# Retention scores and cross terms on the two row halves of the array, 64 deep, instead of zero-padded pairs of heads

## The chip, the cores and the metric

The kernel runs on one core of a Trainium2 chip. The metric is the device time of one execution in microseconds (us). Below, PE is TensorE, DVE is VectorE, ACT is ScalarE, POOL is GpSimd, SP is the queue that issues most transfers. A "weight load" is the LDWEIGHTS in front of every matmul: it puts the stationary operand, up to 128 rows by 128 columns, into the array; the moving operand is then streamed through it, one column after the other.

## The reference, cut to what matters

A hybrid layer: a normalised input is projected, one half of the channels goes through a gated linear recurrence, the other half through chunkwise retention with 8 heads, and an output projection joins them. The change lies in the retention alone:

```python
# q, k: (chunks, 128, 8 heads, 64); v: (chunks, 128, 8 heads, 128)
s = jnp.einsum('bnchd,bnmhd->bnhcm', q, k) * dmask            # scores, inner dimension d = 64
inner = jnp.einsum('bnhcm,bnmhe->bnche', s, v)
kv = jnp.einsum('bnchd,bnche->bnhde', k_dec, v)
state = g_chunk * state + kv                                  # (8 heads, 64, 128), chunk after chunk
cross = jnp.einsum('bnchd,bnhde->bnche', q_dec, state_before) # inner dimension d = 64
o = inner + cross
```

Every product of scores and of cross terms sums over the 64 channels of one head, half of the 128 rows that the array has.

## The kernel before, in words

All large products are made in three passes of a rounded format (float32r): an operand is split into a high part (rounded by ACT) and a low part (the rest, by DVE), and `mm3` (L112 to L116) adds high by high, high by low and low by high into one PSUM bank. The kernel has three stages. Up to about 860 us it makes the recurrence (tiles `px`, `pg`, `pgt`). From there to about 2140 us comes the retention (L619 to L879), and then the output projection (`sweep`, L366).

The retention runs twice over 32 chunks of 128 positions (`for ph in range(2)`, four heads each time: 64 chunk steps in all). One step of the loop at L837 does, for chunk n and the one before it:

- `front_qk` (L696): 24 matmuls of 512 columns project q and k (`ps0`); `rope` (L674) rotates and scales them on DVE.
- `back_s` (L745) of the chunk before: the scores `pS`. `front_g` has transposed q and k, so that a pair of heads stands on the 128 partitions, head 0 on rows 0 to 63 and head 1 on rows 64 to 127. To keep the two heads apart with products of full depth, q was copied into padded tiles `qbh` and `qbl`, 128 rows by 2 x 128 columns, in which each head's rows are zero in the other head's columns. One `mm3` per pair makes 256 columns at once. DVE multiplies by the mask (`sm`, L752).
- `front_v` (L711) and `front_g` (L723): 24 matmuls each for v (`ps1`) and the gate (`ps2`), their copies out, the transposes of q and k by DVE (`pT`, L634), the split into `qh` and `ql`, and the padded copies by ACT (L739 to L742).
- `back_o` (L755): the output `po`. The cross terms are two `mm3` of 256 columns against the padded state `sbh`, `sbl`; the inner terms are four plain float32 products of the masked scores with v (L764), each of which shows as two passes in the trace. Then the chunk's k by v (`pkv`, six matmuls), the update of `state` on DVE (L776), its split by `state_parts` (L638), the statistics of the head norm (L782, L783) and the normalised output `on` (ACT, L791).
- `back_g`, `back_y` (L795, L799): the gate's multiplication, and four transposes `py` on PE.

PSUM has eight banks, two for each of the tags "a" to "d". `ps0` uses "a", `ps1` and `ps2` use "b", `pS` and `py` take turns on "c", and `po` and `pkv` on "d". A tile may be written when the last reader of the tile that had its bank before is done. The order of the instructions on an engine is made by a scheduler that plans with an estimated timeline; the program's text sets only dependences and priorities.

```python
pads: qbh, qbl, sbh, sbl = [P, 2, 2, P] float32r, set to 0 by POOL once (L623 to L628)
mm3(pS[:, 2 * p2:2 * p2 + 2, :], (qh[:, 2 + p2, :], ql[:, 2 + p2, :]), (qbh[:, p2], qbl[:, p2]), True, True)
```

Of the kernel before, what the change touches and what calls it, by code (L numbers as in the profile page):

```python
# [33 lines left out]
def hybrid_kernel(ctx: ExitStack, tc: tile.TileContext, xa, xt, x, meta, w_in, w_out,  # L34
# [584 lines left out]
    with ExitStack() as cd:  # L619
        tp = cd.enter_context(tc.tile_pool(name="cd_t", bufs=2, reuse_waits="tile"))  # L620
        kp = cd.enter_context(tc.tile_pool(name="cd_c", bufs=2, reuse_waits="tile"))

        pads = []  # L623
        for nm in ("qbh", "qbl", "sbh", "sbl"):
            t = kp.tile([P, 2, 2, P], F32R, name=nm, bufs=1)
            nc.gpsimd.memset(t.bitcast(F32), 0.0)
            pads.append(t)
        qbh, qbl, sbh, sbl = pads  # L628

        def transpose4(dst, src):  # L630
            sv = src.rearrange("p (a g e) -> p a g e", a=4, g=4)
# [4 lines left out]
            return ins  # L636

        def state_parts():  # L638
            for j in range(2):
                r = slice(64 * j, 64 * j + 64)  # L640
                nc.scalar.copy(out=sbh[r, :, j, :], in_=state[r])
                nc.vector.tensor_tensor(sbl[r, :, j, :], state[r], sbh[r, :, j, :].bitcast(F32), op=ALU.subtract)

        late = []
        for ph in range(2):
# [77 lines left out]
            def front_g(cur):  # L723
                n = cur["n"]
                pg = proj(2, cur["xs"])
                gs = tp.tile([P, 512], F32, tag="gs", name="gs")
                th = tp.tile([P, 512], F32, tag="th", name="th", bufs=1)
                hr = tp.tile([P, 1], F32, tag="hr", name="hr")
                nc.gpsimd.tensor_scalar(hr, rstd[:, n:n + 1], 0.5, None, op0=ALU.mult)
                nc.scalar.activation(th, pg, AF.Tanh, scale=hr)  # L730
                nc.scalar.activation(gs, pg, AF.Identity, scale=rstd[:, n:n + 1])
                nc.vector.scalar_tensor_tensor(gs, th, 1.0, gs, op0=ALU.add, op1=ALU.mult)
                cur["gs"] = gs
                pT = tp.tile([P, 4, P], F32, tag="pT", name="pT", bufs=1)
                cur["tr"] = transpose4(pT, cur["rd"].rearrange("p h d -> p (h d)"))
                qh = tp.tile([P, 4, P], F32R, tag="qh", name="qh")
                ql = tp.tile([P, 4, P], F32R, tag="ql", name="ql")
                split(pT, qh, ql)
                for j in range(2):  # L739
                    r = slice(64 * j, 64 * j + 64)  # L740
                    nc.scalar.copy(out=qbh[r, :, j, :], in_=pT[r, 0:2, :])
                    nc.scalar.copy(out=qbl[r, :, j, :], in_=ql[r, 0:2, :].bitcast(F32))  # L742
                cur["q"] = (qh, ql)

            def back_s(st):  # L745
                qh, ql = st["q"]
                pS = psp.tile([P, 4, P], F32, tag="c", name="pS")
                for p2 in range(2):
                    mm3(pS[:, 2 * p2:2 * p2 + 2, :], (qh[:, 2 + p2, :], ql[:, 2 + p2, :]),
                        (qbh[:, p2], qbl[:, p2]), True, True)  # L750
                sm = tp.tile([P, 4, P], F32, tag="sm", name="sm")
                nc.vector.tensor_tensor(sm, pS, msk.rearrange("p (h c) -> p h c", c=P), op=ALU.mult)  # L752
                st["sm"] = sm

            def back_o(st):  # L755
                n, sm, v, kn = st["n"], st["sm"], st["v"], st["kn"]
                qh, ql = st["q"]
                po = psp.tile([P, 4, VD], F32, tag="d", name="po")
                for p2 in range(2):
                    mm3(po[:, 2 * p2:2 * p2 + 2, :], (qh[:, p2, :], ql[:, p2, :]), (sbh[:, p2], sbl[:, p2]),  # L760
                        True, False)
                    for j in range(2):
                        h = 2 * p2 + j
                        nc.tensor.matmul(po[:, h, :], sm[:, h, :], v[:, h * VD:(h + 1) * VD],  # L764
                                         start=False, stop=(j == 1))
                if n < NT - 1:
                    vh, vl = st["vs"]
                    pkv = psp.tile([P, 2, 2, VD], F32, tag="d", name="pkv")
                    for p2 in range(2):
                        c = slice(p2 * 128, p2 * 128 + 128)  # L770
                        c2 = slice(p2 * 256, p2 * 256 + 256)
                        mm3(pkv[:, p2], (kn[:, 0, c], kn[:, 1, c]), (vh[:, c2], vl[:, c2]), True, True)
                    for p2 in range(2):
                        for j in range(2):
                            r = slice(64 * j, 64 * j + 64)
                            nc.vector.scalar_tensor_tensor(state[r, p2, :], state[r, p2, :], dc[r, 2, p2:p2 + 1],  # L776
                                                           pkv[r, p2, j, :], op0=ALU.mult, op1=ALU.add)
                    state_parts()
                mv = tp.tile([P, 4, 2], F32, tag="mv", name="mv")
                bs = tp.tile([P, 4, 6], F32, tag="bs", name="bs")  # L780
                for h in range(4):
                    nc.vector.bn_stats(bs[:, h, :], po[:, h, :])  # L782
                    nc.vector.bn_aggr(mv[:, h, :], bs[:, h, :])  # L783
                rs = tp.tile([P, 4], F32, tag="rs", name="rs")
                rsqrt_mean(rs, mv[:, :, 1], P, 4, 1.0)
# [2 lines left out]
                nc.gpsimd.tensor_scalar(nb, nb, -1.0, None, op0=ALU.mult)  # L788
                on = mp.tile([P, 4, VD], F32, tag="xlb", name="on")
                for h in range(4):  # L790
                    nc.scalar.activation(on[:, h, :], po[:, h, :], AF.Identity, bias=nb[:, h:h + 1],  # L791
                                         scale=rs[:, h:h + 1])
                st["on"] = on

# [167 lines left out]
```

## Time and profile before

| | |
|---|---|
| median of 3 runs | 2772.62 us (2769.89 to 2774.16) |
| the profiled execution | 2772.7 us |
| its span, first to last instruction | 2770.9 us |
| PE busy | 2716.7 us, 98% |
| DVE busy | 2130.1 us, 77% |
| ACT busy | 1374.0 us, 50% |
| POOL busy | 544.9 us, 20% |
| mean granted clock of TensorE | 0.994 of full speed |

Matmuls are pipelined: a record lasts longer than the matmul occupies the array, because the next one's record opens while it still drains. So the rows of the timeline are read by their starts: what one matmul costs is the distance from its start to the next one's. Where several records of one line follow one another, the timeline merges them into a row with a count (x8), its start and its whole length. "PEld" rows are weight loads; shapes are rows*columns of the stationary operand, then partitions x columns of the moving one.

### The profile page before, as it was taken

The numbers are of one execution on the slowest core, as the hardware profiler recorded it, in microseconds if no ns is written. First come the engines' busy times: TensorE is split into PE (matmuls) and PEld (weight loads), VectorE is DVE, ScalarE is ACT, GpSimd is POOL, SyncE is SP. The second block draws the span as 40 slices with busy tenths as digits, with TensorE's granted clock in tenths as the row PEclk, the third lists the DMA queues.
The fourth block names the chain that finished last, engine by engine and source line by source line (L and its number), as shares of the span: only waits on it lengthen the run. The fifth ranks groups of instructions, "written<-read, shape, count | busy, mean of one in ns | idle before, by whom it ended". The sixth has DMA issues, their size and how long they took to land.

```text
span 2770.9 us, 37027 instructions
## 1 busy us (share of the span) xinstructions
PE 2716.7 (98%) x13178; PEld 2288.6 (83%) x13178; DVE 2130.1 (77%) x4502; ACT 1374.0 (50%) x2451; POOL 544.9 (20%) x702
## 2 busy tenths in 40 slices
PE   7999999999999999999999999999999999999998
PEld 7788888888888888888888888888887888877886
DVE  7777889878789877777779888888778755566664
ACT  5766666655565444444446544454445422244342
POOL 3101021000003322222222222222221000012222
PEclk9999999999999999999999999999999999999999
DMA  6434334212224222222214222223112745475654
GB/s 197 120 106 121 118 97 122 84 57 67 75 85 145 72 69 72 69 72 69 70 57 164 79 80 83 101 109 114 47 48 77 191 112 111 108 206 162 178 158 116
DMA packets 164411, 290.10 MB, mean 105 GB/s; under 512 B 21201, under 2 KB 89330, under 8 KB 163714
## 3 DMA queue, kind: packets, MB, share of 16 engines
q1 hardware_dynamic: 150690, 238.45, 26.8%
q0 software_dynamic: 13536, 49.29, 8.2%
q8 instruction: 103, 1.69, 0.3%
q14 instruction: 82, 0.67, 0.1%
HBM read 205.87 MB, written 98.58 MB: 110 GB/s over the span
## 4 chain that ended last, share of the span: by engine, by line
PE 80%; DVE 9%; DMA 4%; issue 3%; ACT 2%; POOL 1%; SPq 0%; DVEq 0%; POOLq 0%; ACTq 0%
PE ps L114 12%; PE ps L116 12%; PE ps L115 12%; PE pg L114 3%; PE pg L116 3%; PE pg L115 3%; PE px L116 3%; PE px L114 3%; PE px L115 3%; PE po L764 2%; PE oc L295 2%; PE oc L297 2%; PE od L297 2%; PE oc L296 2%; PE od L296 2%
## 5 line engine op out<-in xcount | busy, mean ns | idle before, releaser
L114 PE MATMUL ps<-cwh,xhi 128*128 128x512 f32 x1536 | 605.7, 394 | 0.6 <-DVE mr L671 0.6
L116 PE MATMUL ps<-cwh,xlo 128*128 128x512 f32 x1536 | 600.4, 391 | 0.7 <-POOL xlo L180 0.7
L115 PE MATMUL ps<-cwl,xhi 128*128 128x512 f32 x1536 | 600.3, 391 | 0.0
L116 PEld LDWEIGHTS ps<-cwh,xlo 128*128 128x128 f32 x1536 | 288.9, 188 | 62.4 <-POOL xlo L180 1.1
L114 PEld LDWEIGHTS ps<-cwh,xhi 128*128 128x128 f32 x1536 | 289.2, 188 | 57.4 <-DVE mr L671 1.0
L115 PEld LDWEIGHTS ps<-cwl,xhi 128*128 128x128 f32 x1536 | 289.2, 188 | 55.8 <-issue 0.2
L634 DVE STREAM_TRANSPOSE pT<-rd 32x128 f32<-32x128 f32 x1024 | 310.0, 303 | 16.4
L180 POOL TENSOR_TENSOR xlo<-xraw,xhi 128x1024 fp32r<-128x1024 f32 x64 | 163.8, 2559 | 529.6 <-ACT xhi L179 523.6
L105 ACT ACTIVATE yop<-yraw 128x512 fp32r<-128x512 f32 x192 | 116.9, 628 | 217.6 <-DVE yraw L264 71.5
L114 PE MATMUL px<-xhi,lwh 128*128 128x512 f32 (+2 forms) x576 | 215.3, 375 | 8.3 <-ACT lwh L108 6.5
L114 PE MATMUL pg<-xhi,lwh 128*128 128x512 f32 (+2 forms) x576 | 212.8, 370 | 3.6 <-DVE sg L492 3.2
L116 PE MATMUL px<-xhi,lwl 128*128 128x512 f32 (+2 forms) x576 | 214.3, 372 | 1.0 <-DVE lwl L106 1.0
L116 PE MATMUL pg<-xhi,lwl 128*128 128x512 f32 (+2 forms) x576 | 212.4, 369 | 2.8 <-DVE lwl L109 1.7
L115 PE MATMUL px<-xlo,lwh 128*128 128x512 f32 (+2 forms) x576 | 213.9, 371 | 1.0 <-DVE xlo L106 0.9
L115 PE MATMUL pg<-xlo,lwh 128*128 128x512 f32 (+2 forms) x576 | 212.2, 368 | 0.0
L475 DVE SCALAR_TENSOR_TENSOR xc<-xlb,vec,xc 128x512 f32<-128x512 f32 (+2 forms) x216 | 155.4, 720 | 30.2 <-ACT xc L472 26.5
L106 DVE TENSOR_TENSOR yop<-yraw,yop 128x512 fp32r<-128x512 f32 x192 | 130.0, 689 | 52.6 <-ACT yop L105 50.7
L791 ACT ACTIVATE on<-po,nb,rs 128x128 f32<-128x128 f32 x256 | 96.3, 457 | 129.7 <-POOL nb L788 129.7
L782 DVE BATCH_NORM_STATS2 bs<-po 128x6 f32<-128x128 f32 x256 | 57.0, 285 | 108.0 <-PE po L764 107.9
L114 PEld LDWEIGHTS px<-xhi,lwh 128*128 128x128 f32 x576 | 110.5, 192 | 26.8 <-ACT lwh L108 6.5
L114 PEld LDWEIGHTS pg<-xhi,lwh 128*128 128x128 f32 x576 | 109.5, 190 | 22.3 <-DVE sg L492 4.3
L115 PEld LDWEIGHTS px<-xlo,lwh 128*128 128x128 f32 x576 | 110.6, 192 | 20.1 <-DVE xlo L106 1.9
(216 smaller groups left out, 6179.8 us busy)
## 6 DMA issues: line engine op xcount, KB each, us to landing
xraw<-in_xt_dram SPq DMA_DIRECT2D x64, 512.0 KB, 4.6
yraw<-ydram SPq DMA_DIRECT2D x64, 512.0 KB, 3.8
xraw<-in_xa_dram SPq DMA_DIRECT2D x56, 512.0 KB, 4.0
hdram<-in_x_dram SPq DMA_DIRECT2D x32, 512.0 KB, 3.9
xn<-in_x_dram SPq DMA_DIRECT2D x32, 512.0 KB, 5.3
ydram<-sg SPq DMA_DIRECT2D x256, 64.0 KB, 1.7
ydram<-yt SPq DMA_DIRECT2D x64, 256.0 KB, 2.4
hdram<-h POOLq DMA_DIRECT2D x32, 512.0 KB, 5.2
```

The source lines that it names most:

```text
L105: nc.scalar.activation(hi, src, AF.Identity)
L106: return nc.vector.tensor_tensor(lo, src, hi.bitcast(F32), op=ALU.subtract)
L114: nc.tensor.matmul(ps, ah, bh, start=start, stop=False)
L115: nc.tensor.matmul(ps, ah, bl, start=False, stop=False)
L116: nc.tensor.matmul(ps, al, bh, start=False, stop=stop)
L180: nc.gpsimd.tensor_tensor(lo, raw, hi.bitcast(F32), op=ALU.subtract)
L296: nc.tensor.matmul(ps, ah, bl, start=False, stop=False, skip_group_check=more)
L297: mm = nc.tensor.matmul(ps, al, bh, start=False, stop=k == 3, skip_group_check=more)
L475: conv = nc.vector.scalar_tensor_tensor(xc[:, :T], xl[:, j:j + T], vec[:, 6 + j, ch:ch + 1], xc[:, :T], op0=ALU.mult, op1=ALU.add)
L634: ins = nc.vector.transpose(dst[32 * g:32 * g + 32, :, 32 * q:32 * q + 32], sv[32 * q:32 * q + 32, :, g, :])
L782: nc.vector.bn_stats(bs[:, h, :], po[:, h, :])
L791: nc.scalar.activation(on[:, h, :], po[:, h, :], AF.Identity, bias=nb[:, h:h + 1], scale=rs[:, h:h + 1])
```

## The change

`back_s` and `back_o` no longer use padded operands. A new helper `pairs3` makes the three products of each head for itself, on 64 rows: head 0 with rows 0 to 63 of both operands, head 1 with rows 64 to 127, in turn. The program places these instructions on the array as tiles of 64 rows by 128 columns, at row 0 and at row 64. Each has 128 moving columns instead of 256, and there are twice as many: 12 for the scores and 12 for the cross terms of a chunk step, where there were 6 and 6. The heads of a pair write different banks, so `pS` and `po` are two tiles each: `pS` takes both banks of "c", `po` both of "d", and `pkv` moves from "d" to "c". The mask is multiplied in two instructions. The inner products (L764 before, L763 now) stand behind all cross terms instead of between them. The padded copies, their zeroing and the halves of the state's split are gone.

```diff
-        pads = []
-        for nm in ("qbh", "qbl", "sbh", "sbl"):
-            t = kp.tile([P, 2, 2, P], F32R, name=nm, bufs=1)
-            nc.gpsimd.memset(t.bitcast(F32), 0.0)
-            pads.append(t)
-        qbh, qbl, sbh, sbl = pads
+        sbh, sbl = [kp.tile([P, 2, VD], F32R, name=nm, bufs=1) for nm in ("sbh", "sbl")]
+        rows = [slice(0, 64), slice(64, 128)]
...
         def state_parts():
-            for j in range(2):
-                r = slice(64 * j, 64 * j + 64)
-                nc.scalar.copy(out=sbh[r, :, j, :], in_=state[r])
-                nc.vector.tensor_tensor(sbl[r, :, j, :], state[r], sbh[r, :, j, :].bitcast(F32), op=ALU.subtract)
+            nc.scalar.copy(out=sbh, in_=state)
+            nc.vector.tensor_tensor(sbl, state, sbh.bitcast(F32), op=ALU.subtract)
+
+        def pairs3(outs, a, b, more=False):
+            for s, (x, y) in enumerate(((0, 0), (0, 1), (1, 0))):
+                for j, r in enumerate(rows):
+                    nc.tensor.matmul(outs[j], a[x][r], b[y][r], start=(s == 0 and not more), stop=(s == 2),
+                                     skip_group_check=True)
...
-                for j in range(2):
-                    r = slice(64 * j, 64 * j + 64)
-                    nc.scalar.copy(out=qbh[r, :, j, :], in_=pT[r, 0:2, :])
-                    nc.scalar.copy(out=qbl[r, :, j, :], in_=ql[r, 0:2, :].bitcast(F32))
                 cur["q"] = (qh, ql)
 
             def back_s(st):
                 qh, ql = st["q"]
-                pS = psp.tile([P, 4, P], F32, tag="c", name="pS")
+                pS = [psp.tile([P, 4, P], F32, tag="c", name="pS") for _ in rows]
                 for p2 in range(2):
-                    mm3(pS[:, 2 * p2:2 * p2 + 2, :], (qh[:, 2 + p2, :], ql[:, 2 + p2, :]),
-                        (qbh[:, p2], qbl[:, p2]), True, True)
+                    pairs3([t[:, p2, :] for t in pS], (qh[:, 2 + p2, :], ql[:, 2 + p2, :]),
+                           (qh[:, p2, :], ql[:, p2, :]), p2 > 0)
                 sm = tp.tile([P, 4, P], F32, tag="sm", name="sm")
-                nc.vector.tensor_tensor(sm, pS, msk.rearrange("p (h c) -> p h c", c=P), op=ALU.mult)
+                mv4 = msk.rearrange("p (a j c) -> p a j c", a=2, j=2)
+                for j, t in enumerate(pS):
+                    nc.vector.tensor_tensor(sm.rearrange("p (a j) c -> p a j c", j=2)[:, :, j, :], t[:, 0:2, :],
+                                            mv4[:, :, j, :], op=ALU.mult)
                 st["sm"] = sm
...
-                po = psp.tile([P, 4, VD], F32, tag="d", name="po")
+                pos = [psp.tile([P, 4, VD], F32, tag="d", name="po") for _ in rows]
+                po = lambda h: pos[h % 2][:, h // 2, :]
                 for p2 in range(2):
-                    mm3(po[:, 2 * p2:2 * p2 + 2, :], (qh[:, p2, :], ql[:, p2, :]), (sbh[:, p2], sbl[:, p2]),
-                        True, False)
-                    for j in range(2):
-                        h = 2 * p2 + j
-                        nc.tensor.matmul(po[:, h, :], sm[:, h, :], v[:, h * VD:(h + 1) * VD],
-                                         start=False, stop=(j == 1))
+                    pairs3([po(2 * p2), po(2 * p2 + 1)], (qh[:, p2, :], ql[:, p2, :]),
+                           (sbh[:, p2], sbl[:, p2]), p2 > 0)
+                for h in range(4):
+                    nc.tensor.matmul(po(h), sm[:, h, :], v[:, h * VD:(h + 1) * VD],
+                                     start=False, stop=True, skip_group_check=True)
                 if n < NT - 1:
                     vh, vl = st["vs"]
-                    pkv = psp.tile([P, 2, 2, VD], F32, tag="d", name="pkv")
+                    pkv = psp.tile([P, 2, 2, VD], F32, tag="c", name="pkv")
```

The scheduler's order on PE at the scores of one chunk step in the first run over the chunks, before (`pS` is the scores' bank, `ps` a projection):

```order
L116 MATMUL ps<-cwh,xlo 128x512
L114 MATMUL pS<-qbh,qh 128x256
L115 MATMUL pS<-qbl,qh 128x256
L116 MATMUL pS<-qbh,ql 128x256
L114 MATMUL pS<-qbh,qh 128x256
L115 MATMUL pS<-qbl,qh 128x256
L116 MATMUL pS<-qbh,ql 128x256
L114 MATMUL ps<-cwh,xhi 128x512
```

The same place now, with buffer numbers (`pS_9797` is head 0 of the pairs, on rows 0 to 63, `pS_9798` head 1, on rows 64 to 127; the rows of the projections stand on both sides as before):

```order
L641 MATMUL pS_9797<-qh_9685 128x128
L641 MATMUL pS_9797<-ql_9686,qh_9685 128x128
L641 MATMUL pS_9798<-qh_9685 128x128
L641 MATMUL pS_9798<-ql_9686,qh_9685 128x128
L641 MATMUL pS_9797<-qh_9685,ql_9686 128x128
L641 MATMUL pS_9798<-qh_9685,ql_9686 128x128
L641 MATMUL pS_9797<-qh_9685 128x128
L641 MATMUL pS_9798<-qh_9685 128x128
L641 MATMUL pS_9797<-ql_9686,qh_9685 128x128
L641 MATMUL pS_9798<-ql_9686,qh_9685 128x128
L641 MATMUL pS_9797<-qh_9685,ql_9686 128x128
L641 MATMUL pS_9798<-qh_9685,ql_9686 128x128
```

Six full-depth products have become twelve of half depth; the first four are ordered head 0, 0, 1, 1 and the others in turn (so in 51 of the 64 chunk steps).

On PE at the output of one chunk step, before (`po` is the output's bank):

```order
L116 MATMUL ps<-cwh,xlo 128x512
L114 MATMUL po<-sbh,qh 128x256
L115 MATMUL po<-sbl,qh 128x256
L116 MATMUL po<-sbh,ql 128x256
L764 MATMUL po<-v,sm 128x128 x2
L114 MATMUL po<-sbh,qh 128x256
L115 MATMUL po<-sbl,qh 128x256
L116 MATMUL po<-sbh,ql 128x256
L764 MATMUL po<-v,sm 128x128 x2
L114 MATMUL pkv<-vh,kn 128x256
```

Now, from the second pair of heads on (six rows like the first six stand ahead, for the first pair; behind the last row `pkv` and `py` go on as before):

```order
L641 MATMUL po_9898<-sbh_7863,qh_9685 128x128
L641 MATMUL po_9899<-sbh_7863,qh_9685 128x128
L641 MATMUL po_9898<-sbl_7864,qh_9685 128x128
L641 MATMUL po_9899<-sbl_7864,qh_9685 128x128
L641 MATMUL po_9898<-sbh_7863,ql_9686 128x128
L641 MATMUL po_9899<-sbh_7863,ql_9686 128x128
L763 MATMUL po_9898<-v_9630,sm_9811 128x128
L763 MATMUL po_9899<-v_9630,sm_9811 128x128
L763 MATMUL po_9898<-v_9630,sm_9811 128x128
L763 MATMUL po_9899<-v_9630,sm_9811 128x128
L114 MATMUL pkv_9916<-vh_9632,kn_9585 128x256
```

The cross terms are one unbroken block of twelve, strictly in turn, and the four inner products stand behind it.

On DVE between the output of one chunk and the scores of the next, now (`state` reads `pkv`'s bank, which the scores of head 1 then get):

```order
L775 SCALAR_TENSOR_TENSOR state<-state,dc,pkv 64x128 x4
L782 BN_AGGR mv<-bs 128x2 x2
L636 TENSOR_TENSOR sbl<-state,sbh 128x256
L685 TENSOR_TENSOR m_9784<-ps_9759,tg 128x512
L688 TENSOR_TENSOR m_9785<-ps_9759,tg 128x8x32 x2
L750 TENSOR_TENSOR sm<-pS,msk 128x2x128 x2
```

The state's update stands, as before, ahead of the rotation of the next q and k (L685); its split is one instruction instead of two, the mask two instead of one.

## Rows read from the trace of the kernel before

**Rows 1.** The page's first part: PE's busy time, share of the span, instructions.

```profile
PE 2716.7 (98%) x13178; PEld 2288.6 (83%) x13178; DVE 2130.1 (77%) x4502; ACT 1374.0 (50%) x2451; POOL 544.9 (20%) x702
```

**Rows 2.** Busy times by stretch: stretch, length, PE, PEld, DVE, ACT, POOL, clock, DMA.

```profile
905.00:1480.00 575.00, 574.79 (x2947) 491.17 (x2946) 450.62 (x1194) 269.50 (x538) 154.94 (x204) 1.00 0.23 74
1560.00:2100.00 540.00, 540.00 (x2769) 462.02 (x2768) 438.69 (x1146) 256.99 (x503) 144.08 (x188) 1.00 0.24 85
```

**Rows 3.** Waits of PE from 905 to 1480 us: total, times, longest, us.

```profile
PE py L804 <- DVE on L797: 0.2, 1, 0.2
```

**Rows 4.** Timeline of PE at the scores of one chunk: start, length, us.

```profile
1207.87 0.29 PE L114 MATMUL pS<-qbh,qh 128*128 128x256 f32 x1
...
1208.60 0.40 PE L114 MATMUL ps<-cwh,xhi 128*128 128x512 f32 x1
```

**Rows 5.** Timeline of PE at the output of the same loop step.

```profile
1219.52 0.29 PE L114 MATMUL po<-sbh,qh 128*128 128x256 f32 x1
...
1219.89 0.61 PE L764 MATMUL po<-v,sm 128*128 128x128 f32 x4
```

**Rows 6.** Timeline of PE, full-array float32 products (L433) between 272-column ones.

```profile
24.43 0.29 PE L116 MATMUL px<-xhi,lwl 128*128 128x272 f32 x1
24.56 0.38 PE L433 MATMUL pr<-idf,rstd 128*128 128x128 f32 x2
...
24.91 0.28 PE L115 MATMUL px<-xlo,lwh 128*128 128x272 f32 x1
```

**Rows 7.** Timeline of PE and PEld, one product on 16 rows (L430).

```profile
23.04 0.29 PE L115 MATMUL px<-xlo,lwh 128*128 128x272 f32 x1
23.16 0.29 PE L116 MATMUL px<-xhi,lwl 128*128 128x272 f32 x1
...
23.93 0.29 PE L115 MATMUL px<-xlo,lwh 128*128 128x272 f32 x1
...
23.38 0.29 PEld L430 LDWEIGHTS pr<-idf,rstd 16*128 16x128 f32 x2
23.70 0.19 PEld L114 LDWEIGHTS px<-xhi,lwh 128*128 128x128 f32 x1
```

**Rows 8.** Line L430 alone: durations ns, min/median/max.

```profile
L430 PEld LDWEIGHTS pr<-idf,rstd x2: 180/182/183, 23.4 to 23.5; 16*128 16x128 f32 x2
```

**Rows 9.** Timeline of PE and PEld, four products on two column halves (L825).

```profile
860.01 0.39 PE L116 MATMUL ps<-cwh,xlo 128*128 128x512 f32 x1
860.24 0.39 PE L114 MATMUL ps<-cwh,xhi 128*128 128x512 f32 x1
860.56 0.65 PE L825 MATMUL pkvm<-mr,rd 16*64 16x128 f32 x8
861.48 0.39 PE L116 MATMUL ps<-cwh,xlo 128*128 128x512 f32 x1
...
860.55 0.41 PEld L825 LDWEIGHTS pkvm<-mr,rd 16*64 16x64 f32 x8 [0.35 <-DVE rd L692]
861.14 0.19 PEld L115 LDWEIGHTS ps<-cwl,xhi 128*128 128x128 f32 x1 [0.17 <-issue]
```

**Rows 10.** Line L825 alone: durations ns, min/median/max.

```profile
L825 PE MATMUL pkvm<-mr,rd x16: 267/268/319, 860.6 to 1508.6; 16*64 16x128 f32 x16
```

**Rows 11.** Groups of instructions from 905 to 1480 us: busy us, mean ns of one, idle before.

```profile
L741 ACT CAST qbh<-pT 64x256 fp32r<-64x256 f32 x57 | 23.1, 405 | 74.0 <-DVE pT L634 73.3
L752 DVE TENSOR_TENSOR sm<-pS,msk 128x512 f32<-128x512 f32 x29 | 19.8, 682 | 0.0
L688 DVE TENSOR_TENSOR m<-ps,tg 128x256 f32<-128x256 f32 x58 | 21.6, 415 | 0.0
```

**Rows 12.** Timeline of POOL, the padded tiles' zeroing, and of DVE and ACT in one chunk step.

```profile
876.81 0.53 POOL L626 MEMSET qbh<- 128x512 f32 x1
...
1203.99 1.41 DVE L776 SCALAR_TENSOR_TENSOR state<-state,dc,pkv 64x128 f32<-64x128 f32 x4
...
1207.96 1.50 ACT L791 ACTIVATE on<-po,nb,rs 128x128 f32<-128x128 f32 x4 [2.08 <-POOL nb L788]
```

More of the change, by code (lines that the diff above doesn't have):

```diff
@@ L781, in back_o @@
                 for h in range(4):
-                    nc.vector.bn_stats(bs[:, h, :], po[:, h, :])
+                    nc.vector.bn_stats(bs[:, h, :], po(h))
                     nc.vector.bn_aggr(mv[:, h, :], bs[:, h, :])
@@ L790, in back_o @@
                 for h in range(4):
-                    nc.scalar.activation(on[:, h, :], po[:, h, :], AF.Identity, bias=nb[:, h:h + 1],
+                    nc.scalar.activation(on[:, h, :], po(h), AF.Identity, bias=nb[:, h:h + 1],
                                          scale=rs[:, h:h + 1])
```

## The prediction

> **What bounds the kernel now.** I read the page's first part, then the busy times by stretch, then the waits, then single instructions. The first part says PE [rows 1]: busy for 98% of the span. That is only a hint, so the next view is the busy time of the two stretches of the retention [rows 2]: PE is busy for 574.79 of 575 us and for 540.00 of 540 us, at a granted clock of 1.00, while DVE has 78% and 81% and ACT less than half. The waits then say whether that is work or waiting in disguise: in 575 us PE waited once, for 0.2 us [rows 3]. So in this stage a microsecond of array time, more or less, is a microsecond of the kernel, and nothing that ACT, DVE or POOL save counts. The change touches PE in 64 chunk steps, all of them in this stage.
>
> **What it removes from PE.** Six matmuls of 256 columns for the scores: from the first `pS` to the next projection, 1207.87 to 1208.60, 0.73 us [rows 4], or 0.12 each. Six for the cross terms: three of them 1219.52 to 1219.89, 0.37 us [rows 5], so 0.73 again. Together 1.46 us a step.
>
> **What it adds to PE.** Twelve matmuls of 64 rows and 128 columns in each place. No row of the trace shows this form, so I take it apart.
>
> First, going into a smaller tile and back. The nearest row is a product on 16 rows and all 128 columns [rows 7]. The 272-column products around it follow each other by 0.12 us (23.04, 23.16). So the array was free at 23.28, but the weight load of the small tile starts at 23.38: 0.10 us of nothing. Normally that load runs beside the matmul before; here it doesn't. Its two loads are 0.11 us apart (0.29 us for both, 0.18 for one alone [rows 7, 8]). After them, at 23.60, the last few columns stream, and the next load, that of the full array, starts at 23.70: 0.09 us of nothing again, and 0.11 us of load until the array streams (the product behind it starts at 23.93, so this one streamed from 23.81). From 23.28 to 23.81 are 0.53 us. Two passes of the same type without a change of tile take 24.55 to 24.79, 0.24 us, though they move eight times the columns [rows 6]. So a round trip costs 0.10 + 0.11 + 0.09 + 0.11 = **0.41 us** around the steps between the first load and the last stream. The four products on column halves agree: the array is free at 860.24 + 0.23 = 860.47 and streams the next full product at 861.48 - 0.23 = 861.25, 0.78 us [rows 9]. By the recipe it is 0.41, less 0.05 for a first load of half the columns, and four steps of 0.11: 0.80.
>
> Second, do two halves work side by side? On column halves they do: eight passes start within 0.65 - 0.27 = 0.38 us [rows 9, 10], 0.05 apart, while a full-array pass of that type takes 0.12 [rows 6]. I take the same for row halves, where no row shows it.
>
> Third, the time between two pairs. The stream alone would be short: 512 columns take 0.23 us [rows 9] and 256 take 0.12 [rows 4], so 128 would take about 0.07 if that line goes on. But each product brings its own 128 weight columns, and loads of 128 columns into the same rows come 0.11 us apart [rows 7, 8]; with 128 columns to stream, the load is the longer. I take 0.11, from the row that is itself a row tile, and keep 0.07 and 0.12 (what float32r products of 256 columns do) as the ends. The Trainium skill, TensorE: Matmul & The Clock Gate, section Back-to-back issue gap, gives about 81 ns for matmuls of 128 columns with their loads, in a long stream; an estimate of the sum by that is 23 us instead of the 44 below, or 2796 us. The 0.11 us between the loads speaks against it here.
>
> The steps: the cross terms stand strictly in turn, six pairs, so five steps and a last stream of 0.06. Of the scores the order has head 0, 0, 1, 1 first: the second product of head 0 comes a load later, head 1 starts with it and stays a product behind, so six steps. Scores: 0.41 + 6 x 0.11 + 0.06 = 1.13 us. Cross terms: 0.41 + 5 x 0.11 + 0.06 = 1.02 us. Against 0.73 each this is 0.40 + 0.29 = **0.69 us more per chunk step**, and 64 of them make 44 us. With 0.07 between pairs it is 0.90 and 0.83, 0.27 a step, 17 us; with 0.12 it is 1.19 and 1.07, 0.80 a step, 51 us.
>
> **What it does to the others.** ACT loses four padded copies of 0.405 us [rows 11] and one half of a split, DVE loses a split's half and gets two masks of about 0.415 (the 256-column row from PSUM) for one of 0.682 [rows 11]. All of it lies under PE's 100%: nothing. POOL's four zeroings of 0.53 us [rows 12] come once; between 0 and 2.1 us, and I take 0. No transfer is added or moved, on SP or POOL. New waits come from the banks. The scores of head 1 get the bank from which the state's update reads; it ends at 1205.40, and the scores start at 1207.87 [rows 4, 12]: 2.4 us to spare, and the order on DVE keeps it ahead of the rotation. The output's banks must be read by `on` before the next output: 1209.46 against 1219.52 [rows 5, 12]. Both cost nothing while this holds. At the ends of the two runs the order breaks some blocks (133 unbroken runs instead of 128): 2 us at most, not counted.
>
> **Sum.** The profiled execution took 2772.7 us, 0.1 above the median of the runs. 2772.7 + 44 = **2817 us**, slower by 1.6%.
>
> **The rivals.**
>
> *The halves take turns.* If row halves don't load or stream beside each other, the change does not do what it says. Twelve loads in a row are 0.41 + 11 x 0.11 + 0.06 = 1.68 us a place, 1.90 us more a step, 122 us: 2894. The same size comes if float32r with only 128 columns streams in two passes like plain float32 (0.11 each [rows 6]): 0.22 a step gives 1.95 and 1.73, 142 us, 2915. For it: no row has two row halves, nor this type with so few columns. Against it: the column halves [rows 9], and the straight line from 512 over 272 to 256 columns.
>
> *The change of tile is free.* The empty 0.10 and 0.09 us stand around tiles of 16 rows. If halves of 64 rows don't empty the array, the first load hides behind the projection before and the round trip goes. Then seven steps and six of 0.07 are 0.49 and 0.42 us: 0.55 less a step, 35 us, **2738 us**. It decides from a round trip under about 0.27 us with steps of 0.07; with steps of 0.11 even a free one gains only 0.03 a step, 2 us, no change. That is the mechanism that the Trainium skill promises in TensorEngine Tiling, section Theoretical Speedup, up to twice for a depth of 64. For it: the pairs do half the columns' work. Against it: both kinds of small tile in this trace pay on the way in and out [rows 7, 9].
>
> **Chances.** The forecast's family, 2790 to 2824: 0.60. Turns or two passes: 0.22. Free change of tile: 0.13, of which 0.09 gain and 0.04 are no change. Something else, such as a bank that comes late or a lower clock: 0.05, slower for the most part. About 0.2%, 5.5 us, can be told from no change. So faster 0.10, same 0.04, slower 0.86. The range for eight in ten has to take in most of the second family: from 2780 to 2900; the likeliest case alone is 2790 to 2824.
>
> **What would show it.** Right: in the changed trace the twelve products start in pairs a few ns apart, pairs 0.11 us apart, a load that starts 0.1 us late at both ends of a block, 1.1 us for a score block, and a PE that waits for nobody. Wrong: single starts 0.1 us apart (turns), pairs 0.07 apart or no empty stretch (free), a projection that starts 0.23 us after the last small product, or a wait of the scores for the state's update (the bank). A granted clock below 1.00 between 905 and 2100 us would be none of these and would break the sum.

## The result and the profile after

The changed kernel takes 2819.62 us, median of 4 runs (2818.18 to 2825.3), against 2773.22 us before on the same chip: a ratio of 1.0168, with a 95% interval of 1.0153 to 1.0182. It is slower by 46 us. The profiled execution of the change has a span of 2818.9 us, that of before 2770.9 us.

The first part of the page, with the busy time of each engine, to be held against [rows 1]:

```profile
PE 2755.7 (98%) x13946; PEld 2285.5 (81%) x13946; DVE 2124.9 (75%) x4502; ACT 1248.0 (44%) x2131; POOL 529.8 (19%) x698
```

The same two stretches as in [rows 2]; the columns are the same:

```profile
905.00:1480.00 575.00, 573.81 (x3210) 474.68 (x3207) 430.28 (x1158) 198.07 (x369) 143.83 (x197) 1.00 0.22 66
1560.00:2100.00 540.00, 540.00 (x3009) 446.39 (x3008) 427.34 (x1113) 199.11 (x358) 134.69 (x185) 1.00 0.24 83
```

ACT lost about a quarter of its work here (269.50 to 198.07 us) and DVE some of its own, and nothing came of it: PE is still the engine that is never idle, at a granted clock of 1.00, and it now has more to do per chunk step. Its waits in the first stretch (line waited for: total, times, longest in us) are again next to nothing:

```profile
PE po L763 <- DVE sm L750: 1.2, 1, 1.2
```

So the time must be inside the products. A score block of the change, in the timeline of PE (start, length, us; "x2" is a pair, one product on each row half):

```profile
1199.86 0.39 PE L116 MATMUL ps<-cwh,xlo 128*128 128x512 f32 x1
1200.18 0.33 PE L641 MATMUL pS<-qh 64*128 64x128 f32 x2
1200.34 0.28 PE L641 MATMUL pS<-ql,qh 64*128 64x128 f32 x2
1200.45 0.28 PE L641 MATMUL pS<-qh,ql 64*128 64x128 f32 x2
1200.57 0.28 PE L641 MATMUL pS<-qh 64*128 64x128 f32 x2
1200.67 0.28 PE L641 MATMUL pS<-ql,qh 64*128 64x128 f32 x2
1200.79 0.28 PE L641 MATMUL pS<-qh,ql 64*128 64x128 f32 x2
1201.00 0.50 PE L114 MATMUL ps<-cwh,xhi 128*128 128x512 f32 x1
```

And the weight loads of the same block:

```profile
1200.17 0.19 PEld L641 LDWEIGHTS pS<-qh 64*128 64x128 f32 x2 [0.35 <-issue]
...
1200.99 0.19 PEld L114 LDWEIGHTS ps<-cwh,xhi 128*128 128x128 f32 x1
```

The 512-column product before the block streams for 0.23 us, from 1199.86 to 1200.09. The first loads of the block start at 1200.17, 0.08 to 0.09 us later. The pairs follow each other by 0.11 us, six of them. The next load of the full array comes at 1200.99, and 0.11 us later, at 1201.10, the array streams again. From 1200.09 to 1201.10 are 1.01 us, for the 0.73 of [rows 4].

The cross terms look the same:

```profile
1212.08 0.33 PE L641 MATMUL po<-sbh,qh 64*128 64x128 f32 x2
...
1212.70 0.27 PE L641 MATMUL po<-sbh,ql 64*128 64x128 f32 x2
1212.90 1.16 PE L763 MATMUL po<-v,sm 128*128 128x128 f32 x8
```

How much that makes per chunk step is read from an instruction that comes once a chunk, ACT's copy of v (L715). These are the rows of that tile for chunks 4, 5 and 28 of before (duration in ns, then first and last start in us):

```profile
L715 ACT ACTIVATE v<-ps,rstd x1: 680/680/680, 937.3 to 937.3; 128x512 f32<-128x512 f32 x1
...
L715 ACT ACTIVATE v<-ps,rstd x1: 680/680/680, 956.1 to 956.1; 128x512 f32<-128x512 f32 x1
...
L715 ACT ACTIVATE v<-ps,rstd x1: 680/680/680, 1413.8 to 1413.8; 128x512 f32<-128x512 f32 x1
```

and for chunks 4 and 28 of the change:

```profile
L715 ACT ACTIVATE v<-ps,rstd x1: 691/691/691, 941.3 to 941.3; 128x512 f32<-128x512 f32 x1
...
L715 ACT ACTIVATE v<-ps,rstd x1: 687/687/687, 1431.4 to 1431.4; 128x512 f32<-128x512 f32 x1
```

Now 24 steps take 490.1 us, 20.42 each, and the single steps are all 20.41 to 20.43. Before, they take 476.5 us, but the first of them is short, 18.8 us, for the most part because only 68 projection products, not 72, fall between its two marks; from chunk 5 to chunk 28 a step takes (1413.8 - 956.1) / 23 = 19.90 us. That is **0.52 us more a step**. Between chunks 35 and 60, in the second run, it is 0.53. Two blocks of 1.01 or 1.02 for two of 0.73 would make 0.56 to 0.58, so a block as read from the starts is some 0.02 us too long. Taken stretch by stretch between such marks (start of the copy of v of the chunk named), the two executions differ by:

| stretch | before, us | after, us | difference |
|---|---|---|---|
| up to the last `px` product, late in the first stage | 831.0 | 831.0 | 0.0 |
| from there to chunk 0 | 28.6 | 28.5 | -0.1 |
| chunk 0 to 4 | 77.7 | 81.8 | 4.1 |
| chunk 4 to 28 | 476.4 | 490.1 | 13.6 |
| chunk 28 to 31 | 60.9 | 62.5 | 1.6 |
| chunk 31 to 35, with the turn to the second run | 87.5 | 94.8 | 7.3 |
| chunk 35 to 60 | 497.0 | 510.1 | 13.2 |
| chunk 60 to the first product of the output stage | 66.7 | 70.4 | 3.7 |
| output stage | 645.0 | 649.7 | 4.7 |

At 0.52 us, 64 steps make 33 us. From chunk 0 to the output stage the change is 43.4 us longer, so the other 10 us lie at the ends of the two runs over the chunks: over 0.52 a step there are 2.0 us in the first four steps, 1.1 in the short step of before, 5.2 at the turn and 1.6 at the end. In the first four steps PE waits twice for masked scores, 2.3 us together, where it had no such wait before. The 4.7 us of the output stage stand apart.

### The profile page after: what moved, and what is told of

It is laid out like the page before. It is cut to its first block, busy times and chain, and to the rows that moved or that the text cites. A ratio compares the mean times of both kernels' runs of the same rounds, so it can differ in the third digit from the quotient of the medians.

```text
span 2818.9 us, 38047 instructions
## 1 busy us (share of the span) xinstructions
PE 2755.7 (98%) x13946; PEld 2285.5 (81%) x13946; DVE 2124.9 (75%) x4502; ACT 1248.0 (44%) x2131; POOL 529.8 (19%) x698
## 4 chain that ended last, share of the span: by engine, by line
PE 73%; DVE 12%; DMA 6%; ACT 4%; issue 3%; SPq 1%; POOL 1%; DVEq 0%; POOLq 0%; ACTq 0%
PE ps L114 12%; PE ps L115 11%; PE ps L116 11%; DMA ydram<-sg 4%; PE po L763 2%; PE oc L295 2%; PE oc L296 2%; PE oc L297 2%; PE od L295 2%; PE od L297 2%; PE od L296 2%; PE pS L641 2%; PE pg L114 2%; PE oa L297 2%; PE oa L295 2%
## 5 line engine op out<-in xcount | busy, mean ns | idle before, releaser
L116 PEld LDWEIGHTS px<-xhi,lwl 128*128 128x128 f32 x576 | 110.3, 192 | 21.0 <-DVE lwl L106 2.3
L116 PEld LDWEIGHTS pg<-xhi,lwl 128*128 128x128 f32 x576 | 109.6, 190 | 21.8 <-DVE lwl L106 2.8
```

Of the source, the lines that this page charges most:

```text
L116: nc.tensor.matmul(ps, al, bh, start=False, stop=stop)
```

## The experiments

The medians below are each set beside the kernel before, run on the same chip (2774 to 2777 us). As the profiled executions differ by up to 5 us before the retention even begins (826.4 to 831.4 us), the step from chunk 4 to chunk 28 (of before, from chunk 5) is the finer measure; it stands in the last column.

| kernel | median, us | ratio to before, 95% | step, us |
|---|---|---|---|
| before | 2773 to 2777 | | 19.90 |
| the change | 2819.6 | 1.0168 (1.0153 to 1.0182) | 20.42 |
| one half, then the other | 2845.1 | 1.0245 (1.0224 to 1.0265) | 20.97 |
| cross terms in two blocks | 2839.3 | 1.0219 (1.0198 to 1.0239) | 20.77 |
| 32 columns | 2815.2 | 1.0137 (1.0114 to 1.0159) | 20.36 |
| one half alone | 2804.1 | 1.0097 (1.0078 to 1.0116) | 20.46 |
| scores only | 2791.9 | 1.0065 (1.0050 to 1.0080) | 20.14 |
| cross terms only | 2796.9 | 1.0079 (1.0064 to 1.0094) | 20.17 |
| one block | 2793.6 | 1.0065 (1.0049 to 1.0082) | 20.12 |
| full depth, 128 columns | 2858.0 | 1.0301 (1.0285 to 1.0316) | 21.14 |
| the change again | 2816.7 | 1.0156 (1.0140 to 1.0172) | 20.42 |
| plain float32, two blocks | 2798.1 | 1.0083 (1.0067 to 1.0099) | 20.10 |
| plain float32, one block | 2762.6 | 0.9961 (0.9948 to 0.9974) | 19.73 |

### Where the seventh step went: one half, then the other

The prediction gave a score block seven load slots (six steps between their starts), because the order has two products of head 0 ahead of head 1. The expectations call that a seventh step. The trace above has six slots, in pairs of like products. So the second half's product must have passed one that waits for the first half. This kernel stretches that to the utmost.

```diff
-        def pairs3(outs, a, b, more=False):
+        def pairs3(outs, a, b, more=False, j=0):
+            r = rows[j]
             for s, (x, y) in enumerate(((0, 0), (0, 1), (1, 0))):
-                for j, r in enumerate(rows):
...
-                for p2 in range(2):
+                for j, p2 in ((0, 0), (0, 1), (1, 0), (1, 1)):
```

> Same twelve products per block as the change, but written one half after the other: six products on rows 0 to 63, then six on rows 64 to 127. Theory A (each half has its own queue, so products on different halves pass each other, as the 6 to 8 ns offsets in the score blocks of the change suggest): six pairs again, 1.02 us a block, 2820 us as the change. Theory B (products start in the order written, as the prediction assumed when it gave the scores a seventh step): only the last of the first half can run beside the first of the second, eleven steps, 0.41 + 10 x 0.11 + 0.06 = 1.57 us a block, 0.55 more x 128 blocks = 70 us, 2890 us. Between the two if the queue is short.

It was neither: 20.97 us a step, 0.55 over the change, 0.28 a block. In the timeline of the weight loads of one block of cross terms:

```profile
1300.36 0.18 PEld L641 LDWEIGHTS po<-sbh,qh 64*128 64x128 f32 x1 [0.35 <-issue]
1300.47 0.19 PEld L641 LDWEIGHTS po<-sbl,qh 64*128 64x128 f32 x1
1300.58 0.19 PEld L641 LDWEIGHTS po<-sbh,ql 64*128 64x128 f32 x1
1300.65 0.23 PEld L641 LDWEIGHTS po<-sbh,qh 64*128 64x128 f32 x2
...
1301.20 0.19 PEld L641 LDWEIGHTS po<-sbh,ql 64*128 64x128 f32 x1
1301.46 0.63 PEld L763 LDWEIGHTS po<-v,sm 128*128 128x128 f32 x5
```

The first half goes 1300.36, .47, .58. At 1300.65 two loads start within 46 ns: the first of the second half, and the fourth of the first half behind it. So the second half starts while three products that were written ahead of it still wait. It passes them, but not all five that wait at the start: 0.28 us are lost, where strict order would have lost 0.55. The blocks of the change itself fill in the rest. Where two products of one half stand ahead of the other half, the halves' first loads are 6 to 7 ns apart; with three ahead 10 ns in five blocks (in two more 266 and 461 ns, which was not followed up); with four ahead 14 ns, in one block; with six ahead 283 ns in nearly every block here. So theory A holds for two products ahead, which is all that the score block of the change needs, in most blocks for three, and in the one block seen for four. Why the limit lies there was not tried.

### The price of going in and out: cross terms in two blocks

```diff
                     pairs3([po(2 * p2), po(2 * p2 + 1)], ...)
-                for h in range(4):
-                    nc.tensor.matmul(po(h), sm[:, h, :], ...)
+                    for h in (2 * p2, 2 * p2 + 1):
+                        nc.tensor.matmul(po(h), sm[:, h, :], ...)
```

> The change with the inner products of scores and values back between the cross terms of the two pairs, so each step enters and leaves the small tile three times, not two. Theory A (a round trip costs 0.41 us, less a step of 0.05 that the two shorter streams give back): 2 x (0.41 + 2 x 0.11 + 0.06) = 1.38 for 1.02 us, 0.36 x 64 = 23 us, about 2843 us. Theory B (the change of tile is free, the cost is the pace of the pairs): 2820 us.

0.35 us more a step than the change, for 0.36 expected; 2839 us. The timeline of PE:

```profile
1295.77 0.27 PE L641 MATMUL po<-sbh,ql 64*128 64x128 f32 x2
1295.97 0.71 PE L763 MATMUL po<-v,sm 128*128 128x128 f32 x4
1296.61 0.33 PE L641 MATMUL po<-sbh,qh 64*128 64x128 f32 x2
...
1296.89 0.28 PE L641 MATMUL po<-sbh,ql 64*128 64x128 f32 x2
1297.10 0.60 PE L763 MATMUL po<-v,sm 128*128 128x128 f32 x3
```

The way out, 0.20 us from the last pair to the first full product (1295.77 to 1295.97), now comes a second time (1296.89 to 1297.10), and so does the way in. The number of the products is unchanged; only the entries a step went from two to three. The rival of a free change of tile falls.

### The same price the other way: one block

Scores and cross terms stand together; the inner products move behind `pkv`, so that the mask has time.

```diff
-                back_s(prev)
                 if cur is not None:
                     front_v(cur)
...
+                back_s(prev)
                 back_o(prev)
...
-                    pkv = psp.tile([P, 2, 2, VD], F32, tag="c", name="pkv")
+                    pkv = psp.tile([P, 2, 2, VD], F32, tag="a", name="pkv")
```

> Scores and cross terms of a step put side by side in one block of twelve pairs, so that the small tile is entered and left once per step, not twice. Theory A (a round trip costs 0.41 us; one block is 0.41 + 11 x 0.11 + 0.06 = 1.68 us for 2 x 1.02): 0.36 x 64 = 23 us less than the change, 2797 us, still 24 over before, since 1.68 is more than 1.46. If the move also ends the waits at the run ends, down to 2786. Theory B (the change of tile is free): 2820 us.

0.30 us less a step than the change, for 0.36 expected; 2793.6 us for 2797. The ends of the block in the timeline of PE:

```profile
1288.26 0.39 PE L116 MATMUL ps<-cwh,xlo 128*128 128x512 f32 x1
1288.58 0.33 PE L641 MATMUL pS<-qh 64*128 64x128 f32 x2
...
1289.18 0.28 PE L641 MATMUL pS<-qh,ql 64*128 64x128 f32 x2
1289.30 0.27 PE L641 MATMUL po<-sbh,qh 64*128 64x128 f32 x2
...
1289.85 0.28 PE L641 MATMUL po<-sbh,ql 64*128 64x128 f32 x2
1290.06 0.39 PE L114 MATMUL pkv<-vh,kn 128*128 128x256 f32 x1
```

From 1288.49 (the product before has streamed its 0.23 us) to 1290.17 (0.11 of load after 1290.06) are 1.68 us, the value expected. From the scores to the cross terms (1289.18 to 1289.30) there is no gap beyond the usual step: the price is that of the change of tile, not of another operand or bank.

### What sets the pace of the pairs: 32 columns

```diff
+                    w = slice(0, P if s == 0 else 32)
-                    nc.tensor.matmul(outs[j], a[x][r], b[y][r], ...)
+                    nc.tensor.matmul(outs[j][:, w], a[x][r], b[y][r][:, w], ...)
```

> The change with only 32 of the 128 columns moved in the second and third of each three products (the correction terms of the other 96 columns are left out). Theory A (the pace of 0.11 us is that of the load of 128 weight columns): nothing changes, 2820 us, pairs still 0.11 us apart. Theory B (it is the pace of 128 float32r columns): four of six steps shrink from 0.11 to 0.03, 0.32 us x 128 blocks = 41 us, 2779 us.

20.36 us a step, 0.06 less than the change; theory B wanted 0.64 less. The timeline of PE:

```profile
1291.37 0.33 PE L642 MATMUL po<-sbh,qh 64*128 64x128 f32 x2
...
1291.61 0.26 PE L642 MATMUL po<-sbh,ql 64*128 64x32 f32 x2
1291.72 0.31 PE L642 MATMUL po<-sbh,qh 64*128 64x128 f32 x2
...
1292.14 0.38 PE L764 MATMUL po<-v,sm 128*128 128x128 f32 x1
```

And two weight loads of the same block, the third and the fourth:

```profile
1291.58 0.19 PEld L642 LDWEIGHTS po<-sbh,ql 64*128 64x128 f32 x2
1291.70 0.19 PEld L642 LDWEIGHTS po<-sbh,qh 64*128 64x128 f32 x2
```

From the first pair to the fourth, 1291.37 to 1291.72, it is 0.35 us, where the change takes 0.39 in its score block (1200.18 to 1200.57), but only because a product that stands behind one of 32 columns starts 0.03 us after the start of its load (1291.70 and 1291.72), where in the change it starts 0.06 after it: the loads themselves stay 0.105 to 0.112 us apart. What is gained is the last stream of each block, 0.03 us. The load of 128 weight columns sets the pace of these float32r products, and with 128 or fewer columns to move the stream lies under it.

### Whether the halves hinder each other: one half alone

```diff
-                for j, r in enumerate(rows):
+                for j, r in list(enumerate(rows))[:1]:
```

The kernel leaves out two of the four heads: their mask reads the other heads' scores, and their output is the inner product alone.

> The change with all products on rows 64 to 127 left out (scores and cross terms of two of the four heads), six products a block on one half. Theory A (the halves load and stream fully side by side): the time of the change, 2820 us, steps of 0.11. Theory B (the pair's loads or streams share something, and a product alone would go faster, in 0.055 us): 6 x 0.055 x 128 = 42 us less, 2778 us.

20.46 us a step, as the change with both halves (20.42); the pairs' second halves are free. The timeline of PE shows single products at the old pace:

```profile
1288.95 0.33 PE L641 MATMUL po<-sbh,qh 64*128 64x128 f32 x1
1289.11 0.27 PE L641 MATMUL po<-sbl,qh 64*128 64x128 f32 x1
```

Half as many products at the same pace also say that the pace does not come from the number of instructions.

The median, 2804 us, lies between the two theories all the same. The steady stretches say A; the difference to the change lies outside them: in the profiles 3 us before the retention, 2 in chunks 0 to 4, 6 at the turn between the runs and 6 in the output stage.

### What the halves are worth at all: full depth, 128 columns

The kernel before, each padded product cut into one per head.

```diff
+                for j in range(2):
+                    nc.tensor.matmul(outs[j], a[x], b[y][:, j, :], ...)
```

> The kernel before with each zero-padded product of 256 columns cut into two of 128: 24 products a step over the full depth for 12, no small tile. Theory A (a product of 128 columns takes the 0.11 us that its 128 weight columns take to load): 24 x 0.11 = 2.64 for 1.46 us, 1.18 x 64 = 76 us, 2849 us. The row halves would then have given 76 us by running two at a time, less the round trips. Theory B (the stream sets the pace, 0.07 us): 24 x 0.07 = 1.68, 14 us, 2787 us.

21.14 us a step, 1.24 over before, and 2858 us. The timeline of PE in a score block:

```profile
1294.93 0.34 PE L647 MATMUL pS<-qbh,qh 128*128 128x128 f32 x2
...
1296.00 0.39 PE L647 MATMUL pS<-qbh,ql 128*128 128x128 f32 x2
```

From the first of the six groups to the last, 1294.93 to 1296.00, ten products start in 1.07 us, 0.107 each; by the step it is (1.46 + 1.24) / 24 = 0.113 us, for 0.12 of one with 256 columns before [rows 4]. This splits the change in two: cutting the products at 128 columns costs 1.24 us a step; putting them on two halves at a time gives back 0.72 (21.14 to 20.42). Padding to 256 columns was nearly free, because a product of 128 columns takes the time of its load, 0.11 us, and one of 256 takes 0.12.

### Each place alone

Scores alone on the row halves (cross terms padded, with the banks of before), and cross terms alone (with the banks of the change).

```diff
 scores only: the cross terms of before
+                    mm3(po[:, 2 * p2:2 * p2 + 2, :], (qh[:, p2, :], ql[:, p2, :]), (sbh[:, p2], sbl[:, p2]), True, False)
 cross terms only: the scores of before
+                    mm3(pS[:, 2 * p2:2 * p2 + 2, :], (qh[:, 2 + p2, :], ql[:, 2 + p2, :]), (qbh[:, p2], qbl[:, p2]), True, True)
```

> Only the scores on the row halves; the cross terms as before, zero padded over the full depth, with the banks as before. The steady step of the change is 0.53 us longer than before, 34 us in 64 steps, and some 12 us more come at the ends of the two runs. Theory A (both blocks cost the same 0.26 us a step and the 12 us hang on the cross terms' side: two banks for the output, the state product in another bank): 2773 + 17 = 2790 us. Theory B (the 12 us hang on the score blocks that are broken up at the ends): 2802 us. Had the scores a seventh step, they alone would cost 0.40 x 64 = 26, 2799 to 2811.

> Only the cross terms on the row halves, with their banks as in the change; the scores zero padded as before. Theory A (as for the scores alone): 2773 + 17 + 12 = 2802 us, with waits for the normalised output at the ends of the runs. Theory B: 2790 us. In either case this and the scores alone should add up to the change: 17 + 17 + 12 = 46 us over before.

0.24 and 0.27 us a step, together 0.51 for the 0.52 of both. The scores cost no more than the cross terms: no seventh step. The medians are 18 and 23 us over before, 41 in all for the 46 of the change (42 in the section that follows), where 64 such steps make 15 and 17: neither side carries the excess at the ends alone, and the question of theory A against B at the ends is not settled by these two.

### The change again

> The change itself once more, for a second profile. Its steady step must be 20.42 us again. Open is the rest: 5 us between the two runs and 4.7 us in the last stage, where one product waited 4.9 us for a residual. If they belong to the change, both come again; if they are chance of one execution, the last stage takes 645 us as before and the total falls by some 4 us.

The step is 20.42 us again. The output stage takes 644.4 us, as before: its 4.7 us were of that one execution. The turn comes again, with 96.5 us from chunk 31 to 35 (94.8 in the first profile, 87.5 before). Over 0.52 a step that is 6.9 us here and 5.2 in the first profile. The waits of PE around the turn in the change's first profile (in this one 2.3 and 1.5 us):

```profile
PE py L803 <- DVE on L796: 2.3, 1, 2.3
PE pkvm L824 <- ACT on L790: 1.2, 1, 1.2
```

The second is a bank that comes late: `pkvm` takes a bank of the output, which `on` reads. Before there was one wait of 1.4 us there, of `py` for `qh`. So the waits explain 2.1 us of the 5.2. In the whole retention four score blocks are broken up, with five more ways in and out of 0.4 us, 2 us in all; three of the five stand at the turn, 1.2 us. And six projection products of 512 columns more than before fall between the two marks (289 and 283), at 0.23 us 1.4 us: there it is the mark that has moved. Half a microsecond is left open.

The 1.7 us by which the turn of this profile is longer come with the granted clock. Here it falls twice to the lower of its two levels (0.50, 1.2 GHz), for 3.4 us each, both times within 1 us of the end of one of the two waits (stretch, length, PE, PEld, DVE, ACT, POOL, clock, DMA):

```profile
1501.94:1505.34 3.40, 3.08 (x10) 2.63 (x11) 3.40 (x9) 3.38 (x7) 0.00 (x0) 0.50 0.00 0
1532.66:1536.06 3.40, 3.40 (x12) 2.73 (x11) 3.37 (x4) 3.33 (x8) 3.06 (x2) 0.50 0.21 77
```

Products of 512 columns follow each other by 0.43 us there, not by 0.23, so one such stretch costs some 1.6 us. In the first profile of the change it falls once at the turn (1505.36 to 1508.76), and so it does before (1509.60 to 1513.00), so that it does not show in the difference of these two.

### A version that beats both

If the number of weight loads on a half sets the time, and not the columns, a product should need few loads. Plain float32 takes two passes per product [rows 6]; three float32r products of split parts take three loads. If on a row half both pace at the load, plain float32 is the cheaper there, and it needs no split of queries or state.

```diff
-        def pairs3(outs, a, b, more=False):
-            for s, (x, y) in enumerate(((0, 0), (0, 1), (1, 0))):
-                for j, r in enumerate(rows):
-                    nc.tensor.matmul(outs[j], a[x][r], b[y][r], ...)
+        def pairs1(outs, a, b, more=False):           # a, b: pT and state, float32
+            for j, r in enumerate(rows):
+                nc.tensor.matmul(outs[j], a[r], b[r], start=not more, stop=True, skip_group_check=True)
```

> The change with plain float32 products on the row halves in place of three float32r products of split parts: each product then runs as two passes, so four pairs a block, not six, and the splits of queries and state go. Theory A (a pair of passes paces at 0.11 us too, as the passes on column halves and the inner products of scores and values do, and the round trip stays 0.41 us): 0.41 + 3 x 0.11 + 0.11 for the last stream = 0.85 us a block, 0.15 less than the 1.00 measured for the change, 0.30 x 64 = 19 us: 2801 us; 15 us over before by blocks alone, and what the run ends add (0 to 12 us). Theory B (plain float32 of 128 columns on half the rows takes twice the load's time, 0.22 us): 0.41 + 4 x 0.22 = 1.29 us a block, 2856 us.

> Plain float32 on the row halves, and scores and cross terms in one block a step. Theory A: 0.41 + 7 x 0.11 + 0.11 = 1.29 us for the 1.46 of before, 0.17 x 64 = 11 us gained, 2762 us, less what the run ends give back (0 to 12 us): 2762 to 2774, so it may beat both kernels or tie with before. Theory B (0.22 us a pass): 0.41 + 8 x 0.22 = 2.17 us, 45 us over before, 2818 us.

Both came out by theory A: 2798 us for 2801 expected, and 2762.6 us for 2762 to 2774. The block of the second in the timeline of PE:

```profile
1275.75 0.39 PE L116 MATMUL ps<-cwh,xlo 128*128 128x512 f32 x1
1276.06 0.72 PE L635 MATMUL pS<-pT 64*128 64x128 f32 x8
1276.61 0.61 PE L635 MATMUL po<-state,pT 64*128 64x128 f32 x8
1277.16 0.39 PE L114 MATMUL pkv<-vh,kn 128*128 128x256 f32 x1
```

From 1275.98 to 1277.27 are 1.29 us, as worked out, for the 1.46 of before. The step is 19.73 us, 0.17 less than before as expected, and 12.6 us, or 0.4%, are gained over before (ratio 0.9961, 0.9948 to 0.9974). Against the change the step falls by 0.69 us, in about equal parts by fewer loads (20.42 to 20.10) and by the one entry (20.42 to 20.12). In the kernel with two blocks a step, seven score blocks between chunks 35 and 60 are broken in two, and the steps there take 20.27 us on average.

That it is the load that paces the plain float32 passes is not shown. On the column halves of [rows 9, 10] such passes have half the weight columns, and the four on each half still start within 0.38 us, 0.13 apart, so their stream of 128 columns may take as long as the load of 128 weight columns does. The sums need only the 0.11 us.

## Why the prediction was right, and where it was not

The forecast was 2817 us, the result 2819.6, in the likeliest case's own range. Point by point:

- **PE is the bound, and what ACT and DVE save counts for nothing: right.** ACT lost 71 us of work in the first stretch and PE stayed at 573.81 of 575 us.
- **The round trip of 0.41 us: right.** It was read from a tile of 16 rows, and holds for 64 rows: one entry more costs 0.35 us a step, one less gives back 0.30, and the recipe's totals of 1.02, 1.68 and 1.29 us were met within 0.02 as read from the starts; by the step a block of the change takes 0.99.
- **Two halves side by side: right.** One half alone has the same step, 20.46 us for 20.42.
- **0.11 us between pairs, from the load: right.** A quarter of the columns leaves it where it was. The Trainium skill, TensorE: Matmul & The Clock Gate, section Back-to-back issue gap, which gives some 81 ns and from which the prediction worked out 2796 us, does not describe these blocks: the loads stay 0.105 to 0.112 us apart. The ceiling of twice the speed that the Trainium skill gives in TensorEngine Tiling (Array Packing), section Theoretical Speedup, is nearly what two halves give, but for the round trips, against products of 128 columns (24 at 0.11 us against 12 pairs at 0.11). It is not reached against the padded products, which were wide enough to need half as many loads.
- **Six steps in a score block, 1.13 us: wrong.** What failed is the sentence that the second product of head 0 comes a load later and head 1 "stays a product behind", that is, that products start in the order written. A product on the other half passes those that wait, so the scores take five steps and 1.01 us, as long as the cross terms. That is 0.11 x 64 = 7 us too much; of the 0.58 that is then left a chunk step, 0.52 was measured, another 4 us, so the 64 steps cost 33 us, not 44.
- **"2 us at most, not counted" for the ends of the runs: wrong.** They cost 10 us in the one profile and 12 in the other, of which 1.7 are the clock's. The broken blocks are the 2 us that it gave. What failed is that it put new waits at nothing: PE waits 2.3 us for masked scores in the first four steps, and at the turn 2.3 for `on` and 1.2 for a bank of the output, where it had 1.4 before. Some 4 of the 10 us are not broken down, and which of the moved banks and orders makes each wait was not tried. The 10 us happen to fill up what the seventh step had put in too much: that the total is nearer than its terms is luck.
- **The rivals.** Turns are excluded by the pairs and by one half alone, two passes by the 0.11 us between pairs, and the free change of tile by the entries. What the halves can lose by their order showed in the experiment of one half after the other, 0.55 us a chunk step, but not in the change.

## What to carry to other kernels

A float32r product of up to 128 columns cost the 0.11 us of its weight load here, not its columns: before cutting a wide padded product into narrow ones on parts of the array, count the loads that each part then has, and keep the wide one if it has fewer. A change of tile has a price at both ends (0.41 us here), so row-tiled products belong in one long block, and the halves need only be mixed to within a few products. At 128 columns a plain float32 pass took no longer than a rounded product, so that two passes were cheaper than three rounded ones (2762.6 us against 2793.6, both with one block).

## What the runs showed of the hardware that was not expected

- Products on different row halves pass each other: with two, three or four of one half ahead, the other half starts 6 to 14 ns behind it (but for two blocks with three ahead); with six ahead, 283 ns.
- A float32r stream of 128 columns hides wholly under a load of 128 weight columns: with a quarter of the columns a block is only 0.03 us shorter.
- A pair of plain float32 passes on the two halves also follows the next by 0.11 us, no slower than a pair of float32r products with the same 128 columns.
